# Start of a batched-experts kernel: x in three loads, and the identity and ScalarE's table load inside the Tile frame

## The chip, the cores and the metric

The kernel runs on one core of a Trainium2 chip. The metric is the device time of one execution in microseconds.

## The reference

Eight experts each have their own x (256 rows of 512), w1 (512 x 2048) and w2 (2048 x 512), all float32. Each expert is two matrix products with a relu between them:

```python
h = np.matmul(x, w1)        # x: (8, 256, 512), w1: (8, 512, 2048)
h = np.maximum(h, 0)
return np.matmul(h, w2).astype(np.float32)   # w2: (8, 2048, 512)
```

## The kernel before

The kernel is written by hand, engine by engine, with its own semaphores. Only its first instructions stand inside a Tile frame: a block that the Tile layer opens and that `tc.close()` ends (L97). At the end of the frame all five engines meet twice, and only then do they go on to the hand-written part. Inside the frame SP issues two loads of x, experts 0 and 1 (L92, first one) and experts 2 and 3 (second one), into `x_f` as float32. The name of each of these instructions is entered in `tc.no_tile_sem_insts`, so that the frame doesn't wait for them; they count up `s_x[0]` and `s_x[1]`.

After the frame:

- **GpSimd's queue (POOL)** issues everything that is cast on the way from float32 to bfloat16: first x of experts 4 to 7 into `x_c` (L139), then w1 of experts 0 and 1 (L129), then it makes the identity (memset L142, select L144, with the semaphore `s_id` between them and after them), then w2 of experts 0 and 1 (L134). w1 and w2 are double-buffered by expert; the later ones are issued when a half of the buffer is free (`s_first`, `s_act`). Last comes the store of experts 0 to 3 of the output (L163).
- **SP's queue**, after the x loads, waits for each weight to land and passes that on to TensorE as tokens (`t_w`, L113 to L121), and stores experts 4 to 6 (L123) and 7 (L125) of the output.
- **VectorE and ScalarE** first prepare x (`take_x`): in four rounds VectorE takes an even expert and ScalarE an odd one, copies it with its rows reordered into `x_b` as bfloat16 (`cast`, L174), waits for TensorE's transposes and copies these out of PSUM into `xe` (L190, and L193 for experts 4 to 7). ScalarE's first instruction here brings a load of its function table with it. Then both run `layers`: the relu out of PSUM into `ht` (L214, L216) and the copies of the output (L223).
- **TensorE** waits for the identity (`s_id`, L246), then makes four rounds of 16 transposes, each of which takes two tokens of `t_xb`, one from either cast. Then for each pair of experts it does the first products (L267) and the second ones (L287).

In `take_x` the wait for a load of x is by round:

```python
if r < G // 2:
    eng.wait_ge(s_x[r], 16)
```

Of the kernel before, what the change touches and what calls it, by code (L numbers as in the profile page):

```python
# [9 lines left out]
def kernel(  # L10
# [7 lines left out]
    nc = tc.nc  # L18
    P = 128
    bf = mybir.dt.bfloat16  # L20
    f32 = mybir.dt.float32
    relu = mybir.ActivationFunctionType.Relu
# [8 lines left out]
    G = E // 2  # L31
# [10 lines left out]
    x_r = x.rearrange("e (p m) k -> p e m k", m=MT)  # L42
# [3 lines left out]
    x_f = nc.alloc_sbuf_tensor("x_f", [P, G, MT, H], f32)  # L46
# [7 lines left out]
    w1_k = w1_sb[:, :2 * KT1 * F].rearrange("p (k n) -> p k n", n=F)  # L54
    w2_k = w2_sb[:].rearrange("p (k n) -> p k n", n=H)
    o_sb = nc.alloc_sbuf_tensor("out_sb", [P, E, MT, H], f32)
    identity = nc.alloc_sbuf_tensor("identity", [P, P], bf)
    ph = [nc.alloc_psum_tensor(f"pt_h{b}", [P, FB // 2, C], f32) for b in range(2)]
    po = nc.alloc_psum_tensor("pt_o", [P, MT, H], f32)
    pt = [nc.alloc_psum_tensor(f"pt_tr{b}", [P, KT1 * MT, P], bf) for b in range(2)]  # L60

    sem = nc.alloc_semaphore
    s_x = [sem(f"s_x{i}") for i in range(G // 2)]
    s_xc = sem("s_xc")
    s_out = [sem(f"s_out{i}") for i in range(3)]
    s_w1 = [sem(f"s_w1_{e}") for e in range(E)]
    s_w2 = [sem(f"s_w2_{e}") for e in range(E)]
    s_w2b = [sem(f"s_w2b_{e}") for e in range(E - 2, E)]
    s_id = sem("s_id")
    s_act = sem("s_act")  # L70
    s_dve = sem("s_dve")
    s_tr = sem("s_tr")
# [11 lines left out]
    sp, pool, act, dve, pe = nc.sync, nc.gpsimd, nc.scalar, nc.vector, nc.tensor  # L84
# [3 lines left out]

    def load_x(e, n, i):
        ins = sp.dma_start(x_f[:, e:e + n], x_r[:, e:e + n]).then_inc(s_x[i], 16)  # L92
        return ins.ins.name

    for r in range(G // 2):
        tc.no_tile_sem_insts.add(load_x(2 * r, 2, r))
    tc.close()  # L97
    tc.compile()  # L98

# [28 lines left out]
    def load_w1(e):  # L128
        pool.dma_start(w1_k[:, e % 2 * KT1:(e % 2 + 1) * KT1], w1_r[e]).then_inc(s_w1[e], 16)  # L129

    def load_w2(e):
        k = e % 2 * KT2
        if e < E - 2:
            pool.dma_start(w2_k[:, k:k + KT2], w2_r[e]).then_inc(s_w2[e], 16)  # L134
        else:
            pool.dma_start(w2_k[:, k:k + CUT], w2_r[e, :, :CUT]).then_inc(s_w2[e], 16)  # L136
            pool.dma_start(w2_k[:, k + CUT:k + KT2], w2_r[e, :, CUT:]).then_inc(s_w2b[e - E], 16)
# [1 line left out]
    pool.dma_start(x_c[:], x_rows).then_inc(s_xc, 16)  # L139
    load_w1(0)  # L140
    load_w1(1)
    pool.memset(identity[:], 0.0).then_inc(s_id, 1)  # L142
    pool.wait_ge(s_id, 1)
    pool.affine_select(  # L144
        out=identity[:],
        in_=identity[:],
        compare_op=mybir.AluOpType.not_equal,
        fill=1.0,
        base=0,
        pattern=[[-1, P]],  # L150
        channel_multiplier=1,
    ).then_inc(s_id, 1)
    load_w2(0)
    load_w2(1)
    for e in range(2, E, 2):
# [13 lines left out]
    def cast(eng, r, b):  # L169

        a = 2 * r + b
        src = x_f[:, a] if a < G else x_c[:, MT * (a - G):MT * (a - G + 1)]
        copy = act.copy if eng is act else dve.tensor_copy
        copy(  # L174
            x_b[:, b].rearrange("p (t m) q -> p t m q", m=MT),
            src.rearrange("p m (q t) -> p t m q", t=KT1),
        ).then_inc(t_xb, 1)

    def take_x(eng, b):
        copy = act.copy if eng is act else dve.tensor_copy  # L180
        for r in range(G):
            if r < G // 2:
                eng.wait_ge(s_x[r], 16)
            elif r == G // 2:
                eng.wait_ge(s_xc, 16)
            cast(eng, r, b)
            eng.wait_ge(s_tr, 2 * r + b + 1)
            a, n = 2 * r + b, KT1 * C
            if a < G:
                copy(xe[:, a * n:(a + 1) * n], pt[b][:].rearrange("p j q -> p (j q)")).then_inc(s_xe[b], 1)  # L190
            else:
                xl = xe[:, G * n:].rearrange("p (l j q f) -> p l j q f", l=G, j=KT1 * MT, f=G)
                copy(  # L193
                    xl[:, :, :, :, a - G].rearrange("p l j q -> p j l q"),
                    pt[b][:].rearrange("p j (l q) -> p j l q", l=G),
                ).then_inc(s_xe[b], 1)
# [28 lines left out]

    act.sem_inc(t_ha, 1)
    take_x(act, 1)
    layers(act, 1, s_ha, s_oa, t_ha, s_act)

    dve.sem_inc(t_hb, 1)  # L230
    take_x(dve, 0)
    layers(dve, 0, s_hb, s_ob, t_hb, s_dve)

# [9 lines left out]
            pe.lower_ap(aps[-1], for_matmul_weights=weights)  # L243
        return aps

    pe.wait_ge(s_id, 2)  # L246
    with pe.Fori(0, G) as _r:
        take(t_xb, 2)
        for b in range(2):
            for j in range(KT1 * MT):  # L250
                ins = pe.transpose(pt[b][:, j], x_b[:, b, j], identity[:])  # L251
            ins.then_inc(s_tr, 1)

    with pe.Fori(0, G) as g:
        with pe.Fori(0, 2) as b:
            xs = ahead(xe, False, g * (4 * KT1 * C) + b * (2 * KT1 * C), [kt * C for kt in range(KT1)], C)
            take(t_w)
            with pe.Fori(0, NQ) as q:
                for i in range(FB):
# [6 lines left out]
                    for kt in range(KT1):  # L266
                        ins = pe.matmul(  # L267
                            ph[i // 2][:, i % 2, :],
                            ws[i % 2 * KT1 + kt],
                            xs[kt],  # L270
                            start=(kt == 0),
                            stop=(kt == KT1 - 1),
                        )
                    if i % 2:
                        ins.then_inc((s_hb, s_ha)[i // 2], 1)
        with pe.Fori(0, 2) as b:
            for kt in range(KT2):
# [8 lines left out]
                for m in range(MT):  # L286
                    ins = pe.matmul(  # L287
                        po[:, m],
                        hs[(kt - k0) * MT + m],
                        ws[kt - k0],  # L290
                        start=(kt == 0),
                        stop=(kt == KT2 - 1),
                    )
# [35 lines left out]
```

## Time and profile before

| | before |
|---|---|
| median of 3 runs | 179.58 us (179.54 to 179.58) |
| profiled execution, its own time | 179.67 us |
| its span, first to last instruction | 178.4 us |
| mean granted TensorE clock | 0.963 of full |
| TensorE matmul busy | 131.5 us (74%) |
| VectorE, ScalarE, GpSimd busy | 37.3, 37.9, 12.4 us |
| read from and written to HBM | 71.30 MB and 4.19 MB, 423 GB/s over the span |
| share of the software DMA queue (GpSimd's) | 94.2% of the 16 DMA engines' span |

A row of the profile names an engine, a line of the kernel, an operation, and what it writes and reads (`x_f<-in_x_dram`); "PEq", "SPq" and the like are the sequencers of the engines. Times are microseconds from the first instruction. `w_sb` stands for both weight buffers, `pt_tr`, `pt_h` and `pt_o` for the PSUM tensors of the transposes, of the first and of the second products.

### The profile page before, as it was taken

Reading aid. Unit: us, or ns where it says so; the run is one execution under the profiler, and the core shown is the slowest. Engines: PE = TensorE matmul, PEld = TensorE weight load, DVE = VectorE, ACT = ScalarE, POOL = GpSimd, SP = SyncE. Lnnn points to the kernel's source line nnn. Section 1 sums busy time; section 2 is a strip of 40 time slices with the busy share of each in tenths; the row PEclk is TensorE's granted clock in tenths of the full one; section 3 lists DMA queues with packets and bytes.
Section 4 is the critical chain, followed back from the end, with each engine's and each line's share of the span. In section 5 each row is a group of like instructions: output and inputs, shape, how many; then the busy total and the mean of one; then the engine's idle time right before and its main releaser. Section 6 shows DMA issues by size and latency. Waiting matters only on the chain. (4 is left out here: it accounts for less than half of the span.)

```text
span 178.4 us, 2360 instructions
## 1 busy us (share of the span) xinstructions
PE 131.5 (74%) x832; PEld 89.3 (50%) x832; DVE 37.3 (21%) x48; ACT 37.9 (21%) x49; POOL 12.4 (7%) x26
## 2 busy tenths in 40 slices
PE   0214479899949696899769695979495695998950
PEld 0213368796413295794224485954142694953410
DVE  0232653332010133131100231320101141311010
ACT  2455554222010122121100132220101122311010
POOL 3500000101010101001000101010202100000000
PEclk9999999999987999699969999999999999999996
DMA  5999989989989989989999998998998999999998
GB/s 181 349 234 235 228 184 235 235 176 235 235 176 235 235 184 228 235 191 220 235 206 206 235 220 191 235 232 180 235 235 176 235 235 192 201 214 225 280 417 353
DMA packets 4352, 40.90 MB, mean 229 GB/s; under 512 B 384, under 2 KB 384, under 8 KB 2176
## 3 DMA queue, kind: packets, MB, share of 16 engines
q0 software_dynamic: 3264, 36.70, 94.2%
q1 hardware_dynamic: 1088, 4.19, 6.1%
HBM read 71.30 MB, written 4.19 MB: 423 GB/s over the span
## 5 line engine op out<-in xcount | busy, mean ns | idle before, releaser
L267 PE MATMUL pt_h<-xe,w_sb 128*128 x512 | 65.0, 284 | 12.9 <-PEq L87 12.9
L267 PEld LDWEIGHTS pt_h<-xe,w_sb 128*128 x512 | 57.5, 147 | 21.0 <-issue 19.2
L287 PE MATMUL pt_o<-w_sb,ht_sb 128*128 x256 | 59.7, 393 | 9.7 <-PEq L87 9.7
L287 PEld LDWEIGHTS pt_o<-w_sb,ht_sb 128*128 x256 | 25.3, 100 | 42.7 <-issue 16.2
L216 DVE TENSOR_SCALAR ht_sb<-pt_h 128x512 bf16<-128x512 f32 x32 | 22.1, 692 | 51.7 <-PE pt_h L267 51.6
L214 ACT ACTIVATE ht_sb<-pt_h 128x512 bf16<-128x512 f32 x32 | 19.1, 597 | 56.7 <-PE pt_h L267 56.7
L251 PE MATMUL pt_tr<-identity,x_b 128*128 128x128 bf16 x64 | 7.5, 309 | 17.7 <-PEq L87 17.7
L223 DVE COPY out_sb<-pt_o 128x512 f32 x8 | 5.5, 692 | 66.1 <-PE pt_o L287 66.1
L223 ACT COPY out_sb<-pt_o 128x512 f32 x8 | 4.7, 586 | 64.3 <-PE pt_o L287 64.3
L251 PEld LDWEIGHTS pt_tr<-identity,x_b 128*128 128x128 bf16 x64 | 6.5, 143 | 18.4 <-issue 18.4
L129 POOL DMA_DIRECT2D w_sb<-in_w_dram x8 | 4.3, 534 | 71.3 <-ACTq L218 71.3
L134 POOL DMA_DIRECT2D w_sb<-in_w_dram x6 | 3.9, 652 | 35.3 <-ACT out_sb L223 35.2
L193 DVE COPY xe<-pt_tr 128x1024 bf16<-128x1024 bf16 x2 | 4.9, 2466 | 5.2 <-PE pt_tr L251 5.2
L193 ACT COPY xe<-pt_tr 128x1024 bf16<-128x1024 bf16 x2 | 4.9, 2465 | 4.1 <-PE pt_tr L251 4.1
L174 ACT CAST x_b<-x_f 128x1024 bf16<-128x1024 f32 x2 | 4.0, 2000 | 2.9 <-DMA x_f<-in_x_dram 2.9
L174 DVE CAST x_b<-x_f 128x1024 bf16<-128x1024 f32 x2 | 2.2, 1076 | 7.9 <-DMA x_f<-in_x_dram 7.9
L190 ACT COPY xe<-pt_tr 128x1024 bf16<-128x1024 bf16 x2 | 2.0, 1012 | 4.1 <-PE pt_tr L251 4.1
L190 DVE COPY xe<-pt_tr 128x1024 bf16<-128x1024 bf16 x2 | 1.4, 692 | 4.2 <-PE pt_tr L251 4.2
L136 POOL DMA_DIRECT2D w_sb<-in_w_dram x2 | 1.1, 531 | 17.0 <-ACT out_sb L223 17.0
L174 ACT COPY x_b<-x_c 128x1024 bf16<-128x1024 bf16 x2 | 2.2, 1118 | 0.0
L174 ACT ACT_TABLE_LOAD x1 | 1.3, 1283 | 2.6 <-PEq L98 2.6
L174 DVE COPY x_b<-x_c 128x1024 bf16<-128x1024 bf16 x2 | 1.4, 700 | 0.0
(9 smaller groups left out, 3.4 us busy)
## 6 DMA issues: line engine op xcount, KB each, us to landing
w_sb<-in_w_dram POOLq DMA_DIRECT2D x14, 2048.0 KB, 29.5
w_sb<-in_w_dram POOLq DMA_DIRECT2D x2, 1152.0 KB, 26.7
x_f<-in_x_dram SPq DMA_DIRECT2D x2, 1024.0 KB, 7.7
out_dram<-out_sb POOLq DMA_DIRECT2D x1, 2048.0 KB, 36.0
w_sb<-in_w_dram POOLq DMA_DIRECT2D x2, 896.0 KB, 30.4
out_dram<-out_sb SPq DMA_DIRECT2D x1, 1536.0 KB, 8.6
x_c<-in_x_dram POOLq DMA_DIRECT2D x1, 1024.0 KB, 9.9
out_dram<-out_sb SPq DMA_DIRECT2D x1, 512.0 KB, 5.8
```

The source lines that it names most:

```text
L129: pool.dma_start(w1_k[:, e % 2 * KT1:(e % 2 + 1) * KT1], w1_r[e]).then_inc(s_w1[e], 16)
L134: pool.dma_start(w2_k[:, k:k + KT2], w2_r[e]).then_inc(s_w2[e], 16)
L136: pool.dma_start(w2_k[:, k:k + CUT], w2_r[e, :, :CUT]).then_inc(s_w2[e], 16)
L174: copy(x_b[:, b].rearrange("p (t m) q -> p t m q", m=MT), src.rearrange("p m (q t) -> p t m q", t=KT1),).then_inc(t_xb, 1)
L190: copy(xe[:, a * n:(a + 1) * n], pt[b][:].rearrange("p j q -> p (j q)")).then_inc(s_xe[b], 1)
L193: copy(xl[:, :, :, :, a - G].rearrange("p l j q -> p j l q"), pt[b][:].rearrange("p j (l q) -> p j l q", l=G),).then_inc(s_xe[b], 1)
L214: act.activation(dst, ph[half][:], relu).then_inc(t_h, 1)
L216: dve.tensor_relu(dst, ph[half][:]).then_inc(t_h, 1)
L223: copy(outs[b], po[:, half]).then_inc(s_copied, 1)
L251: ins = pe.transpose(pt[b][:, j], x_b[:, b, j], identity[:])
L267: ins = pe.matmul(ph[i // 2][:, i % 2, :], ws[i % 2 * KT1 + kt], xs[kt], start=(kt == 0), stop=(kt == KT1 - 1),)
L287: ins = pe.matmul(po[:, m], hs[(kt - k0) * MT + m], ws[kt - k0], start=(kt == 0), stop=(kt == KT2 - 1),)
```

## The change

SP issues three loads of x in the frame instead of two: expert 0 alone, expert 1 alone (128 rows of 4 KB each), and experts 2 and 3 together. In the first round VectorE waits for expert 0's load and ScalarE for expert 1's, in the second both wait for the third. In the frame ScalarE runs a relu on one column of a constant, `warm`, which brings the table load with it, and GpSimd makes the identity. The semaphore `s_id` and TensorE's wait for it are gone; the frame itself orders the select behind the memset, with a semaphore that Tile allocates. In the built program that semaphore is cleared by GpSimd between the two meetings at the frame's end, and SP waits for it there.

```diff
+    warm = nc.alloc_sbuf_tensor("warm", [P, 1], f32)
...
-    s_x = [sem(f"s_x{i}") for i in range(G // 2)]
+    s_x = [sem(f"s_x{i}") for i in range(3)]
...
-    s_id = sem("s_id")
...
+    def own(ins):
+        tc.no_tile_sem_insts.add(ins.ins.name)
+
     def load_x(e, n, i):
-        ins = sp.dma_start(x_f[:, e:e + n], x_r[:, e:e + n]).then_inc(s_x[i], 16)
-        return ins.ins.name
-
-    for r in range(G // 2):
-        tc.no_tile_sem_insts.add(load_x(2 * r, 2, r))
+        own(sp.dma_start(x_f[:, e:e + n], x_r[:, e:e + n]).then_inc(s_x[i], 16))
+
+    for i, (e, n) in enumerate(((0, 1), (1, 1), (2, 2))):
+        load_x(e, n, i)
+    act.activation(warm[:], nc.const_aps.tensor(1.0, [P, 1], f32), relu)
+    pool.memset(identity[:], 0.0)
+    pool.affine_select(
+        out=identity[:],
+        in_=identity[:],
+        compare_op=mybir.AluOpType.not_equal,
+        fill=1.0,
+        base=0,
+        pattern=[[-1, P]],
+        channel_multiplier=1,
+    )
     tc.close()
     tc.compile()
...
     load_w1(0)
     load_w1(1)
-    pool.memset(identity[:], 0.0).then_inc(s_id, 1)
-    pool.wait_ge(s_id, 1)
-    pool.affine_select(
-        ...
-    ).then_inc(s_id, 1)
     load_w2(0)
     load_w2(1)
...
             if r < G // 2:
-                eng.wait_ge(s_x[r], 16)
+                eng.wait_ge(s_x[b if r == 0 else 2], 16)
...
-    pe.wait_ge(s_id, 2)
     with pe.Fori(0, G) as _r:
```

More of the change, by code (lines that the diff above doesn't have):

```diff
@@ L141 @@
     load_w1(1)
-    pool.memset(identity[:], 0.0).then_inc(s_id, 1)
-    pool.wait_ge(s_id, 1)
[L144 to L151, printed above, removed]
-    ).then_inc(s_id, 1)
     load_w2(0)
```

## The prediction

> **What bounds the kernel now.** The page comes first: how busy each engine is, how busy the DMA engines are, and what the queues carried.
>
> ```profile
> span 178.4 us, 2360 instructions
> PE 131.5 (74%) x832; PEld 89.3 (50%) x832; DVE 37.3 (21%) x48; ACT 37.9 (21%) x49; POOL 12.4 (7%) x26
> DMA  5999989989989989989999998998998999999998
> q0 software_dynamic: 3264, 36.70, 94.2%
> HBM read 71.30 MB, written 4.19 MB: 423 GB/s over the span
> w_sb<-in_w_dram POOLq DMA_DIRECT2D x14, 2048.0 KB, 29.5
> ```
>
> TensorE is busy for three quarters of the span, the DMA engines for nearly all of it. To see whether they ever stand still, I cut the span where the traffic changes (the columns after the stretch are its length, the five engines, the granted clock, the DMA share and GB/s written at the destination; a weight is read as float32 and written as bfloat16, so its GB/s count half of what is read).
>
> ```profile
> 0.00:1.70 1.70, 0.00 (x0) 0.00 (x0) 0.00 (x0) 0.00 (x0) 0.20 (x4) 1.00 0.00 0
> 1.70:2.70 1.00, 0.00 (x0) 0.00 (x0) 0.00 (x0) 0.15 (x1) 0.00 (x0) 1.00 0.84 70
> 2.70:6.80 4.10, 0.00 (x0) 0.00 (x0) 1.09 (x1) 2.31 (x2) 3.44 (x6) 1.00 1.02 421
> 6.80:7.60 0.80, 0.00 (x0) 0.00 (x0) 0.00 (x0) 0.80 (x1) 0.57 (x2) 1.00 1.14 307
> 7.60:12.40 4.80, 1.86 (x16) 1.63 (x16) 1.31 (x2) 1.67 (x3) 0.00 (x0) 1.00 1.03 234
> 12.40:168.30 155.90, 126.13 (x801) 86.26 (x802) 34.17 (x45) 32.40 (x45) 8.18 (x15) 0.97 1.02 217
> 168.30:177.60 9.30, 3.54 (x17) 1.40 (x15) 0.69 (x1) 0.59 (x1) 0.00 (x0) 0.88 1.02 420
> 177.60:178.40 0.80, 0.00 (x0) 0.00 (x0) 0.00 (x0) 0.00 (x0) 0.00 (x0) 0.50 0.09 36
> ```
>
> From 2.7 to 177.6 us the share is 1.02 or more in every stretch: there is no hole. The 155.9 us in the middle are the 16 weight matrices, so one takes 9.74 us; the page's 29.5 us from issue to landing are three of those, that is, each matrix is queued about 20 us before its turn. Nothing that TensorE, VectorE or ScalarE does by a microsecond or two earlier or later reaches the weight stream. At the end the writes of the output run at 420 GB/s to 0.8 us before the end of the span. So the time is: when the DMA engines start, plus any hole in their work, plus a fixed amount of bytes. A step of the change counts only if it moves the start (1.8 us) or opens a hole.
>
> **The change part by part.** All of it lies in the first eight microseconds. This is the timeline there (start, duration, engine, line, operation), and the issue durations of the x loads and of the two output stores that SP issues:
>
> ```profile
> 0.74 0.95 SPq L92 DMA_DIRECT2D x_f<-in_x_dram  x2
> 2.55 1.28 ACT L174 ACT_TABLE_LOAD   x1 [2.55 <-PEq L98]
> 2.99 0.68 POOL L139 DMA_DIRECT2D x_c<-in_x_dram  x1 [2.54 <-POOLq L98]
> 3.66 1.07 POOL L129 DMA_DIRECT2D w_sb<-in_w_dram  x2
> 4.70 0.24 POOL L142 MEMSET identity<- 128x128 bf16 x1
> 5.18 0.28 POOL L144 TENSOR_SCALAR_AFFINE_SELECT identity<-identity 128x128 bf16<-128x128 bf16 x1 [0.24 <-POOL identity L142]
> 5.63 2.01 ACT L174 CAST x_b<-x_f 128x1024 bf16<-128x1024 f32 x1 [1.79 <-DMA x_f<-in_x_dram]
> 5.63 1.09 DVE L174 CAST x_b<-x_f 128x1024 bf16<-128x1024 f32 x1 [5.63 <-DMA x_f<-in_x_dram]
> L92 SPq DMA_DIRECT2D x_f<-in_x_dram x2: 433/446/459, 0.7 to 1.2; - x2
> 168.48 0.39 SPq L123 DMA_DIRECT2D out_dram<-out_sb  x1
> 172.49 0.36 SPq L125 DMA_DIRECT2D out_dram<-out_sb  x1
> ```
>
> *Three x loads for two.* The bytes are the same. Expert 0 arrives alone after 0.52 MB instead of with expert 1 after 1.05 MB, at 421 GB/s some 1.25 us sooner, so VectorE's cast starts near 4.4 instead of 5.63. That gains nothing by itself: TensorE's first transposes take two casts, and ScalarE's, on expert 1, still starts when expert 1 has landed, near 5.6, and takes 2.01 us. The start of traffic stays: the first issue still begins at 0.74. Its duration could shrink from 433 ns to the 0.36 us of L125, which has 128 rows, so data could come 0.07 us sooner; but L123 with 384 rows takes 0.39, less than the 256-row loads, so the row count isn't what sets it. I take 0, bounds -0.07 and +0.05 (the end marks of one more transfer).
>
> *The frame's end moves.* SP issues three loads before it reaches the end of the Tile frame, at which all engines meet. Now it is through at 0.74 + 0.95 = 1.69, and GpSimd's x_c load is issued at 2.99, 1.30 us behind it. A third issue costs 0.36 (L125) to 0.48 us (half of 0.95): SP is through at 2.05 to 2.17.
>
> *The table load in the frame.* ScalarE now loads after the frame (2.55 to 3.83), and then idles 1.79 us for x_f, so nothing is won by moving it. In the frame it begins with SP's first issue, near 0.74, takes 1.28, and the one-column activation follows. The nearest rows for that:
>
> ```profile
> L190 ACT COPY xe<-pt_tr 128x1024 bf16<-128x1024 bf16 x2 | 2.0, 1012 | 4.1 <-PE pt_tr L251 4.1
> L223 ACT COPY out_sb<-pt_o 128x512 f32 x8 | 4.7, 586 | 64.3 <-PE pt_o L287 64.3
> L214 ACT ACTIVATE ht_sb<-pt_h 128x512 bf16<-128x512 f32 x32 | 19.1, 597 | 56.7 <-PE pt_h L267 56.7
> ```
>
> 512 columns more cost 426 ns, so one column costs about 586 - 426 = 160 ns; at most it is the 597 of a whole ACTIVATE. ScalarE reaches the frame's end at 0.74 + 1.28 + 0.16 = 2.18 (at most 2.62): level with SP.
>
> *The identity in the frame.* GpSimd's memset to the end of the select takes 4.70 to 5.46, 0.76 us; in the frame it ends near 1.5, well before SP. Behind the frame 0.9 us of GpSimd's time between the w1 and w2 issues goes away. The w2 load that is then issued sooner has its turn behind x_c and two w1, after 12.4 + 2 x 9.74 = 31.9 us: worth nothing. TensorE loses its wait for the identity, which had passed long before the casts ended (7.64). In the built program the identity makes the frame use a semaphore of its own, and GpSimd clears that between the two meetings at the frame's end while the others arrive there; I take 0 for it, bounds 0 and 0.1 (one of its const memsets takes 0.1).
>
> *Sum for GpSimd's queue.* The x_c load is issued 0.36 to 0.58 us later; I take 0.5, at 3.49. With ScalarE at its bound it would be 0.93 + 0.1. What hides this is the x traffic of SP's queue. Packets and MB by queue, first up to 6.8 us (no packet of the software queue is in that answer), then from 6.8 to 7.2, then up to 13:
>
> ```profile
> q1 hardware_dynamic: 454, 1.79, 74.1%
> ...
> q0 software_dynamic: 12, 0.10, 117.0%
> ...
> q1 hardware_dynamic: 544, 2.10, 44.9%
> ```
>
> At 6.8 us SP's loads have 2.10 - 1.79 = 0.31 MB to go, which at 421 GB/s last 0.74 us, to 7.54. In the profile shown x_c's first packets start at 6.8, 3.81 us behind their issue. If that lag stays, they start at 7.30 now (7.16 to 7.38; at the far bound 7.83). 7.30 is before 7.54: the DMA engines work through, with x_f first and x_c after it instead of mixed. **Hole: 0** (far bound 7.83 - 7.54 = 0.29). If the cover were gone, the whole 0.5 us would show in the time.
>
> The sum against the profiled execution: its own time is 179.67 us, span 178.4 and 1.27 around it; plus 0 for the start, 0 for the hole, and 0 for all that hangs behind the weights. That execution stands 0.09 above the median of the runs shown, 179.58, so I give 179.6. The likeliest case alone spans 179.5 to 179.9 (-0.07 for the start; +0.29 for the hole).
>
> **A rule that speaks against the change.** VectorE's cast now begins at 4.4, when GpSimd is just done with x_c's descriptors (3.49 + 0.68 = 4.17) and at work on w1's. That this matters is seen in one row, the w2 issues, whose first, at 5.59, lies beside the cast of 5.63 to 6.72:
>
> ```profile
> 5.59 1.78 POOL L134 DMA_DIRECT2D w_sb<-in_w_dram  x2
> L134 POOL DMA_DIRECT2D w_sb<-in_w_dram x6: 531/531/1248, 5.6 to 100.0; - x6
> ```
>
> One of six took 1248 ns instead of 531, and 5.59 + 1.25 = 6.84, 0.12 us behind the end of the cast: the issue stood still while VectorE cast. Here w1 is what stands still, to about 4.4 + 1.09 + 0.12 = 5.6, and its turn is at 12.4, so I cost it at nothing. The Trainium skill ("SBUF — State Buffer", section "SBUF: two separate sides") states that GpSimd can't write descriptors while VectorE holds their shared port in a 2-port mode, and that a float32 tensor_copy within SBUF triggers it; by that rule, and on the times above, the sum stays as it is, as long as x_c's descriptors are written first. The trace's 1248 ns agree with it.
>
> **The rivals.** *Slower: the cast catches x_c's descriptors.* If x_c's issue slips 0.9 us rather than 0.5 (ScalarE at its bound of 0.93 does it), it is still being written when the cast starts at 4.4; the point of decision is a slip of 0.7 (2.99 + 0.68 + 0.7 = 4.4). Then it ends at 5.6 instead of 3.67, the first packets come at 5.6 + (6.8 - 3.67) = 8.7, and the hole is 8.7 - 7.54 = 1.2 us: 180.8 us. For it: the 1248 ns and the small margin, 0.2 us by my sum. Against it: x_c's first packets at 6.8 stand so close to the end of the cast, 6.72, that the lag of 3.8 us may itself be partly this wait, in which case an earlier cast releases x_c earlier.
>
> *Slower: ScalarE holds the frame's end.* If the frame's end has to wait after a table load as long again as the load itself, ScalarE arrives at 0.74 + 2 x 1.28 + 0.16 = 3.46, 1.77 later than SP does now; x_c's packets start at 6.8 + 1.77 = 8.57, the hole is 1.0: 180.6 us. The trace can't tell: after its load ScalarE idles 1.79 us for x_f anyway. The Trainium skill ("ScalarE: Activation LUTs", section "What ACT_TABLE_LOAD costs") gives 1283 ns for the load, as the trace has it, and a drain of about 1380 ns behind it, which no row here shows; if that drain were additional, an estimate from its figures is a hole of 1.1 us.
>
> *Faster: the first data come sooner.* From the first issue to data are 1.8 - 0.74 = 1.06 us. If that were proportional to the rows of the transfer, 128 instead of 256 would save 0.5 us, and every byte behind would come as much sooner: 179.1. Against it, 384 rows are issued in 0.39 and 128 in 0.36.
>
> *The change does nothing at all:* the frame's end might not move, if SP's issues overlap with it. That is 179.6 too.
>
> **How the numbers follow.** 0.2% is 0.36 us, about what a measurement of this kernel can tell from no change. The forecast and the case that nothing moves, both inside it: 0.62. The cast catching x_c: 0.16. ScalarE at the frame's end: 0.06. A lag or slip beyond my bounds without either of these, hole 0.4 to 0.9: 0.07. First data sooner: 0.09. So faster 0.09, same 0.62, slower 0.16 + 0.06 + 0.07 = 0.29. The range runs from 179.2, leaving out most of the faster case, to 180.8, which holds the two slower rivals; it is wide because one cause of 0.2 us can turn a hidden slip into a hole of a microsecond.
>
> **What would show it.** Right: SP's three issues end near 2.1; the table load starts near 0.74; x_c is issued near 3.5; the expert 0 cast starts near 4.4 and ScalarE's near 5.6; no stretch from 2.7 us to the last 0.8 us has a DMA share clearly under 1; the last ACT copy of the tail (now 171.88) stays within 0.3 us. Wrong: x_c's issue lasting clearly over 0.68 us, or x_c's first packets later than 7.6 with a low DMA share before them, and the first weight matmul of each later expert late by the same amount; or x_f data before 1.5 us.

## The result, and the profile after

| | before | changed |
|---|---|---|
| median of 12 runs | 179.6 us (179.45 to 179.96) | 180.23 us (179.53 to 181.22) |
| ratio, 95% interval | | 1.0037 (1.0021 to 1.0053) |
| profiled execution: time, span | 179.67, 178.4 us | 181.06, 179.7 us |

The changed kernel is 0.37% slower (0.2 to 0.5), 0.63 us by the medians; the forecast was 179.6, no change. The median hides what happens: six of the twelve runs lie between 179.53 and 179.86 like the kernel before, the other six between 180.59 and 181.22. The profiled execution is one of the slower six.

The page of the changed kernel, in the lines that answer to those of before:

```profile
span 179.7 us, 2356 instructions
DMA  5999999999999999999999999999999999999996
q0 software_dynamic: 3264, 36.70, 93.5%
HBM read 71.30 MB, written 4.19 MB: 420 GB/s over the span
x_f<-in_x_dram SPq DMA_DIRECT2D x1, 1024.0 KB, 8.1
x_c<-in_x_dram POOLq DMA_DIRECT2D x1, 1024.0 KB, 11.1
```

The bytes are the same, and at this grain the DMA row shows nothing. Its start, in the timeline:

```profile
0.74 0.20 POOL L100 MEMSET identity<- 128x128 bf16 x1 [0.29 <-POOLq L314]
0.74 1.28 ACT L99 ACT_TABLE_LOAD   x1 [0.74 <-PEq L314]
0.74 1.34 SPq L95 DMA_DIRECT2D x_f<-in_x_dram  x3
1.02 0.29 POOL L101 TENSOR_SCALAR_AFFINE_SELECT identity<-identity 128x128 bf16<-128x128 bf16 x1
2.04 0.20 ACT L99 ACTIVATE warm<-const-float32-1.0 128x1 f32<-128x1 f32 x1
3.48 0.67 POOL L152 DMA_DIRECT2D x_c<-in_x_dram  x1 [2.18 <-POOLq L111]
4.12 1.07 DVE L176 CAST x_b<-x_f 128x1024 bf16<-128x1024 f32 x1 [4.12 <-DMA x_f<-in_x_dram]
4.15 1.69 POOL L142 DMA_DIRECT2D w_sb<-in_w_dram  x2
5.33 1.99 ACT L176 CAST x_b<-x_f 128x1024 bf16<-128x1024 f32 x1 [3.09 <-DMA x_f<-in_x_dram]
```

Each of these times is where the prediction put it, within 0.3 us. What it missed is in the windows (stretch, length, five engines, granted clock, DMA share, GB/s):

```profile
2.30:3.40 1.10, 0.00 (x0) 0.00 (x0) 0.00 (x0) 0.00 (x0) 0.00 (x0) 1.00 1.01 402
3.40:4.60 1.20, 0.00 (x0) 0.00 (x0) 0.48 (x1) 0.00 (x0) 1.12 (x2) 1.00 1.04 427
4.60:5.40 0.80, 0.00 (x0) 0.00 (x0) 0.59 (x1) 0.07 (x1) 0.80 (x2) 1.00 0.57 205
5.40:6.60 1.20, 0.00 (x0) 0.00 (x0) 0.00 (x0) 1.20 (x1) 1.20 (x3) 1.00 0.79 304
6.60:7.40 0.80, 0.00 (x0) 0.00 (x0) 0.00 (x0) 0.72 (x1) 0.29 (x1) 1.00 1.02 328
```

Three of the same cuts of the kernel before:

```profile
2.30:3.40 1.10, 0.00 (x0) 0.00 (x0) 0.00 (x0) 0.85 (x1) 0.41 (x1) 1.00 0.68 276
4.60:5.40 0.80, 0.00 (x0) 0.00 (x0) 0.00 (x0) 0.00 (x0) 0.56 (x3) 1.00 1.05 430
5.40:6.60 1.20, 0.00 (x0) 0.00 (x0) 0.97 (x1) 0.97 (x1) 1.07 (x2) 1.00 1.02 420
```

There is a hole from 4.6 to 6.6 us: share 0.57 and then 0.79, 205 and 304 GB/s instead of 430 and 420. At 4.6 us the first two x loads have used up their bytes, and the third isn't there yet on many of the DMA engines: by the packets in the trace, about half of the 16 are moving a row at 5.0 us, where in the kernel before all are. Lost are 0.8 x 225 + 1.2 x 116 = 319 KB, 0.76 us at 420 GB/s; a sooner start gave back 1.1 x 126 = 139 KB. The mean loss is smaller than the time, because every transfer is complete only when the slowest DMA engine has done its part, and the holes are not shared evenly: x_c lands at 3.48 + 11.1 = 14.6 us instead of 2.99 + 9.9 = 12.9, 1.7 us later. The 9.9 is in the page of the kernel before:

```profile
x_c<-in_x_dram POOLq DMA_DIRECT2D x1, 1024.0 KB, 9.9
```

Thirteen of the 16 parts of x_c land by 13.6 us, the other three at 14.4 to 14.6; in the kernel before all sixteen land at 12.7 to 12.9. The delay of the latest three goes on nearly unchanged through all weights to the last copies of the output, first in the changed kernel, then in the kernel before:

```profile
166.40 7.07 PE L288 MATMUL pt_o<-w_sb,ht_sb 128*128 x31 [0.79 <-PEq L87]
173.50 0.58 ACT L225 COPY out_sb<-pt_o 128x512 f32 x1 [7.27 <-PE pt_o L288]
```

```profile
171.88 0.59 ACT L223 COPY out_sb<-pt_o 128x512 f32 x1 [7.27 <-PE pt_o L287]
```

173.50 against 171.88 is 1.62 us; the span is 1.3 longer.

### The profile page after: what moved, and what is told of

Read it like the earlier page. It is cut to its first block, busy times and chain, and to the rows that moved or that the text cites. A ratio compares the mean times of both kernels' runs of the same rounds, so it can differ in the third digit from the quotient of the medians.

```text
span 179.7 us, 2356 instructions
## 1 busy us (share of the span) xinstructions
PE 134.7 (75%) x824; PEld 91.2 (51%) x832; DVE 37.3 (21%) x48; ACT 37.9 (21%) x50; POOL 12.3 (7%) x26
## 5 line engine op out<-in xcount | busy, mean ns | idle before, releaser
L268 PE MATMUL pt_h<-xe,w_sb 128*128 x512 | 68.1, 293 | 12.6 <-PEq L87 12.5
L268 PEld LDWEIGHTS pt_h<-xe,w_sb 128*128 x512 | 59.4, 148 | 22.1 <-issue 18.9
## 6 DMA issues: line engine op xcount, KB each, us to landing
x_c<-in_x_dram POOLq DMA_DIRECT2D x1, 1024.0 KB, 11.1
```

The source lines that it names most:

```text
L268: ins = pe.matmul(ph[i // 2][:, i % 2, :], ws[i % 2 * KT1 + kt], xs[kt], start=(kt == 0), stop=(kt == KT1 - 1),)
```

## The experiments

Each is an edit of the changed kernel unless it says otherwise. The ratios are to the kernel before, timed beside them.

**VectorE's cast late.** Is it the third load, VectorE's early cast, or the later frame end?

```diff
-                eng.wait_ge(s_x[b if r == 0 else 2], 16)
+                if r == 0:
+                    eng.wait_ge(s_x[0], 16)
+                eng.wait_ge(s_x[1 if r == 0 else 2], 16)
```

> The changed kernel, but VectorE waits for experts 0 and 1 both before its first cast, so that the cast starts near 5.3 us instead of 4.1; the three x loads and the frame stay. Theory A (the third x load reaches some DMA engines late because it is the third one outstanding in SP's queue): the hole in the DMA work at 4.6 to 6.6 us stays, runs scatter from 179.5 to 181.2, median near 180.2. Theory B (VectorE's early cast, beside GpSimd's descriptor writing, makes the hole): no hole, share 1.0 from 2.3 us on, times 179.2 to 179.6 with little scatter. Theory C (the later frame end and x_c issue make it): as in A.

Median 180.53 us (179.72 to 181.14, six of eight runs over 180), ratio 1.0041 (1.0021 to 1.0061). The cast starts at 5.43 and the hole stays; these are windows of this kernel:

```profile
4.60:5.00 0.40, 0.00 (x0) 0.00 (x0) 0.00 (x0) 0.00 (x0) 0.40 (x2) 1.00 0.60 195
5.00:5.40 0.40, 0.00 (x0) 0.00 (x0) 0.00 (x0) 0.00 (x0) 0.40 (x2) 1.00 1.01 225
```

That is 195 and 225 GB/s where the kernel before has 430. The share of 1.01 beside 225 GB/s isn't full work: by the packets in the trace, nine rows that begin between 5.0 and 5.6 us take 0.42 to 1.11 us each, where most take 0.16. So the early cast is not the cause.

**One and three experts.**

```diff
-    for i, (e, n) in enumerate(((0, 1), (1, 1), (2, 2))):
+    for i, (e, n) in enumerate(((0, 1), (1, 3))):
...
-                eng.wait_ge(s_x[b if r == 0 else 2], 16)
+                eng.wait_ge(s_x[b if r == 0 else 1], 16)
```

> The changed kernel with two x loads instead of three: expert 0 alone, experts 1 to 3 together. VectorE's first cast stays early (near 4.1 us), ScalarE's first cast moves to near 7.8. Theory A: only two loads, no hole, 179.2 to 179.6. Theory B: the early cast still lies beside GpSimd's descriptor writing, hole near 4.6 to 6.6 us, scatter up to 181. Theory C: x_c's issue goes back to near 3.0 us, no hole.

179.6 us (179.49 to 179.87), ratio 0.9997 (0.9989 to 1.0006). The early cast (4.14) and the table load in the frame stay; with two loads there is no slow half. My line on x_c's issue was wrong: it is at 3.43, not 3.0, though SP is through at 1.61, 0.47 us sooner than with three loads.

**Two loads as before, the rest in the frame.**

```diff
-    for i, (e, n) in enumerate(((0, 1), (1, 1), (2, 2))):
+    for i, (e, n) in enumerate(((0, 2), (2, 2))):
...
-                eng.wait_ge(s_x[b if r == 0 else 2], 16)
+                eng.wait_ge(s_x[r], 16)
```

> The changed kernel with the two x loads of the kernel before (experts 0 and 1, experts 2 and 3); identity and table load stay in the frame. Theories A and B: no hole, 179.6 like the kernel before, since the first full DMA rate is back at 2.7 us and the cast back at 5.6. Theory C: the frame's part alone shows, if ScalarE or the semaphore clear hold the frame's end: x_c issued at 3.2 or later, and a slower median by 0.1 to 0.6.

179.71 us (179.51 to 179.95), ratio 1.0003 (0.9994 to 1.0012): the frame's part costs nothing that shows. But it does move the frame's end:

```profile
0.74 1.28 ACT L99 ACT_TABLE_LOAD   x1 [0.74 <-PEq L314]
0.74 0.95 SPq L95 DMA_DIRECT2D x_f<-in_x_dram  x2
2.04 0.20 ACT L99 ACTIVATE warm<-const-float32-1.0 128x1 f32<-128x1 f32 x1
3.42 0.67 POOL L152 DMA_DIRECT2D x_c<-in_x_dram  x1 [2.12 <-POOLq L111]
```

SP is through at 1.69, as before; ScalarE ends at 2.24, and x_c is issued 1.18 us behind that, at 3.42 instead of 2.99. The frame's part alone moves x_c's issue by 0.43 us, and x_f's traffic hides it, as the prediction's sum had it.

**Three loads alone**, the other half of the change put on the kernel before:

```diff
-    for r in range(G // 2):
-        tc.no_tile_sem_insts.add(load_x(2 * r, 2, r))
+    for i, (e, n) in enumerate(((0, 1), (1, 1), (2, 2))):
+        tc.no_tile_sem_insts.add(load_x(e, n, i))
...
-                eng.wait_ge(s_x[r], 16)
+                eng.wait_ge(s_x[b if r == 0 else 2], 16)
```

> The kernel before with only the x loads changed to three (expert 0, expert 1, experts 2 and 3); identity and table load stay behind the frame. Theories A and B: the hole at 4.6 to 6.6 us and the scatter up to 181.2, median near 180.2, as in the changed kernel. Theory C: no hole, 179.2 to 179.6.

180.66 us (179.69 to 181.03, eight of twelve over 180), ratio 1.0038 (1.0022 to 1.0055): the whole of the change's loss. A window shows the same hole:

```profile
4.60:5.00 0.40, 0.00 (x0) 0.00 (x0) 0.40 (x1) 0.00 (x0) 0.40 (x1) 1.00 0.42 154
```

**The third load from ScalarE's queue.**

```diff
-    for i, (e, n) in enumerate(((0, 1), (1, 1), (2, 2))):
+    for i, (e, n) in enumerate(((0, 1), (1, 1))):
...
     act.activation(warm[:], nc.const_aps.tensor(1.0, [P, 1], f32), relu)
+    own(act.dma_start(x_f[:, 2:4], x_r[:, 2:4]).then_inc(s_x[2], 16))
```

> The changed kernel, but the third x load (experts 2 and 3) is issued by ScalarE's queue, in the frame behind the table load (near 2.3 us), instead of SP's. Theory L (a queue keeps two loads going, the third starts about a microsecond or more after the first has landed): no queue has more than two, so no hole at 4.6 to 6.6 us, times 179.4 to 179.8. Theory S (a load needs 2.6 to 4.5 us from its issue to its data under traffic, and the two short loads before it cover only to 4.7): issued 0.6 us later than by SP, the hole stays or grows, median 180.2 or more.

179.53 us (179.46 to 179.69), ratio 0.9991 (0.9982 to 1.0): no hole. But the load wasn't issued behind the table load, as I had expected:

```profile
0.81 0.44 ACTq L100 DMA_DIRECT2D x_f<-in_x_dram  x1
```

ScalarE's sequencer issued it at 0.81 while the table was being loaded. So it was there early, and this run says that a second queue cures the hole, not whether the cure is the queue or the earlier issue. Its trace shows something more: from 4.2 to 5.1 us every packet is of ScalarE's load, 0.35 MB, and none of SP's second load, whose issue was over at 1.60 and whose forerunner had landed by 4.45. So here even the second load comes a while behind its turn; whether it was late or had to wait for the other queue, the trace doesn't tell, but the other queue's traffic fills the time.

**Four loads of one expert.**

```diff
-    for i, (e, n) in enumerate(((0, 1), (1, 1), (2, 2))):
+    for i, (e, n) in enumerate(((0, 1), (1, 1), (2, 1), (3, 1))):
...
-                eng.wait_ge(s_x[b if r == 0 else 2], 16)
+                eng.wait_ge(s_x[2 * r + b], 16)
```

> The changed kernel with four x loads of one expert each. Theory L: the third starts late as before (hole from 4.6 us) and the fourth again waits for the second, so the hole is as large or larger, median 180.2 to 181. Theory S: the fourth is issued near 2.1 us and has arrived by 6.6, so one hole as in the changed kernel, median near 180.2 to 180.5. If neither, no hole: 179.6. The frame's end also moves by 0.45 us, x_c issued near 3.9.

180.82 us (180.34 to 180.93, all five runs slow), ratio 1.0056 (1.0042 to 1.0069), but by another cause than either theory's. From its timeline and its windows:

```profile
3.94 1.54 POOL L152 DMA_DIRECT2D x_c<-in_x_dram  x1 [2.64 <-POOLq L111]
4.30 1.06 DVE L176 CAST x_b<-x_f 128x1024 bf16<-128x1024 f32 x1 [4.30 <-DMA x_f<-in_x_dram]
```

```profile
7.40:12.40 5.00, 1.86 (x16) 1.62 (x16) 1.67 (x2) 2.96 (x3) 0.20 (x1) 1.00 0.89 184
```

At 4.6 us nothing like the hole of the changed kernel is seen (369 GB/s from 4.6 to 5.4). The fourth issue moves x_c's to 3.94, VectorE's cast starts at 4.30 while its descriptors are written, the issue lasts 1.54 us instead of 0.67, and the hole comes where x_f ends. This is the prediction's slower rival, which the change as made just misses (x_c's issue is over at 4.15, the cast starts at 4.12, and it lasted 0.67).

**Four loads, cast late.** To see whether that is it, the cast was made to wait for expert 1 as well:

```diff
-                eng.wait_ge(s_x[2 * r + b], 16)
+                if r == 0:
+                    eng.wait_ge(s_x[0], 16)
+                eng.wait_ge(s_x[1 if r == 0 else 2 + b], 16)
```

> Four x loads of one expert each as in the run before it, but VectorE's first cast waits for expert 1 too and so starts near 5.4 us, behind x_c's descriptors (issue near 3.9 to 4.6). If the cast that caught x_c's descriptors was what made that run slow (its x_c issue lasted 1.54 us instead of 0.67): x_c's issue takes 0.67 again, x_c lands near 13 on all DMA engines, 179.5 to 179.8. If four loads are slow by themselves: 180.3 to 180.9 again.

179.66 us (179.51 to 180.76), ratio 1.0011 (0.9998 to 1.0024).

```profile
3.94 0.68 POOL L152 DMA_DIRECT2D x_c<-in_x_dram  x1 [2.64 <-POOLq L111]
5.45 1.07 DVE L176 CAST x_b<-x_f 128x1024 bf16<-128x1024 f32 x1 [5.45 <-DMA x_f<-in_x_dram]
```

```profile
7.40:12.40 5.00, 1.87 (x16) 1.63 (x16) 1.67 (x2) 2.93 (x3) 0.00 (x0) 1.00 1.13 238
```

Its timeline and window show that the issue is at 3.94 as before, takes 0.68 again, and the hole behind it is gone: by the medians the collision is worth 180.82 - 179.66 = 1.16 us (the kernel before had a median of 179.70 beside both). But four of the twelve runs lie at 180.01 to 180.76: third and fourth loads of 128 rows may still be late at times. None of these four was profiled, so that isn't shown.

**Two, one and one expert; one, two and one.** Three loads, with the long one first or in the middle (waits to match):

```diff
-    for i, (e, n) in enumerate(((0, 1), (1, 1), (2, 2))):
+    for i, (e, n) in enumerate(((0, 2), (2, 1), (3, 1))):
```

> The changed kernel with three x loads in another order of size: experts 0 and 1 together, then expert 2, then expert 3. The third is issued at 1.7 us as in the changed kernel and needed near 6.4. Theory L: the first lands near 5.6, so the third starts at 6.3 to 8: a hole from 6.4, partly filled by x_c's packets from 7.3 on; median 179.8 to 180.5. Theory S: 2.6 to 4.5 us from its issue it is there (4.3 to 6.2), so no hole, 179.6.

179.72 us (179.57 to 180.22), ratio 1.0005 (0.9996 to 1.0014); ten of eleven runs show no loss, and the eleventh wasn't profiled. The hole that theory L as I had put it (third load at 6.3 to 8 us) called for is not there.

```diff
-    for i, (e, n) in enumerate(((0, 1), (1, 1), (2, 2))):
+    for i, (e, n) in enumerate(((0, 1), (1, 2), (3, 1))):
```

> The changed kernel with three x loads: expert 0, then experts 1 and 2 together, then expert 3. The second lasts until about 6.0 us. Theory L: the first lands near 4.1, the third starts from 4.7 to 6.6: covered by the second but for the latest DMA engines, median 179.6 to 179.9. Theory S: the same. If any third load costs a fixed hole: 180.2 or more.

179.55 us (179.37 to 179.84), ratio 0.9993 (0.9984 to 1.0002). Three loads as such cost nothing. With the second load lasting until about 6, the third is in time in every run, and the sooner start is kept: the interval just reaches 1, so a gain isn't shown.

**Halves.** Meant to tell theory L from a limit on the rows in the queue:

```diff
-    for i, (e, n) in enumerate(((0, 1), (1, 1), (2, 2))):
-        load_x(e, n, i)
+    for i in range(2):
+        h = slice(64 * i, 64 * i + 64)
+        own(sp.dma_start(x_f[h, 0:1], x_r[h, 0:1]).then_inc(s_x[i], 16))
+    load_x(1, 1, 2)
+    load_x(2, 2, 3)
```

> The changed kernel with the first load in two halves of 64 rows (expert 0), then expert 1, then experts 2 and 3; VectorE's first cast waits for the first three. Theory L (two loads of a queue at a time): the third waits for the first half, hole from 3.5 us, and again from 4.7; DMA share clearly under 1 at 3.5 to 4.0. Theory K (a queue holds a limited number of rows, 34 marks per DMA engine and not 35, so that the last load of 256 rows waits for room): nothing at 3.5, the last load waits only for the first half, which is over near 2.9, so a small hole or none at 4.7; time 179.5 to 180.0.

181.07 us (180.54 to 181.85), ratio 1.0073 (1.0047 to 1.0099), and inconclusive, since with the halves the traffic behind the first 0.5 us is slow by itself:

```profile
2.30:3.40 1.10, 0.00 (x0) 0.00 (x0) 0.00 (x0) 0.00 (x0) 0.00 (x0) 1.00 0.77 231
3.40:4.60 1.20, 0.00 (x0) 0.00 (x0) 0.00 (x0) 0.00 (x0) 0.18 (x1) 1.00 1.00 222
```

A share of 1.00 at 222 GB/s is no hole, but DMA engines that are busy and move half as much: a row that begins between 3.4 and 4.6 us takes some 0.25 to 0.32 us instead of 0.16. The 231 GB/s of the first window, at a share of 0.77, are the start-up: from 2.7 to 3.2 us the first half itself runs at 369.

**The changed kernel twice more**, for its profile:

> The changed kernel again, for a second profile. If the hole at 4.6 to 6.6 us is what makes the scatter: a time near 181 with the hole, or a time of 179.5 to 179.9 without it.

> The changed kernel once more, for a third profile; the same expectation as the run before.

One came out slow, 181.12 us, one quick, 179.58. First the slow one, by windows and by the issues of its page (the last column is the time from issue to landing):

```profile
4.60:5.40 0.80, 0.00 (x0) 0.00 (x0) 0.53 (x1) 0.11 (x1) 0.80 (x2) 1.00 1.00 312
5.40:6.60 1.20, 0.00 (x0) 0.00 (x0) 0.00 (x0) 1.20 (x1) 1.20 (x3) 1.00 0.94 369
```

```profile
x_f<-in_x_dram SPq DMA_DIRECT2D x1, 1024.0 KB, 13.8
x_c<-in_x_dram POOLq DMA_DIRECT2D x1, 1024.0 KB, 11.2
```

The quick one, by the same two views:

```profile
4.60:5.40 0.80, 0.00 (x0) 0.00 (x0) 0.69 (x1) 0.00 (x0) 0.80 (x2) 1.00 1.05 420
5.40:6.60 1.20, 0.00 (x0) 0.00 (x0) 0.00 (x0) 1.14 (x1) 1.20 (x4) 1.00 1.01 416
```

```profile
x_f<-in_x_dram SPq DMA_DIRECT2D x1, 1024.0 KB, 6.6
x_c<-in_x_dram POOLq DMA_DIRECT2D x1, 1024.0 KB, 9.5
```

The quick one has no hole at all; its third x load is complete 6.6 us after the issue, and x_c 9.5. In the slow one they take 13.8 and 11.2. The hole is smaller on average here than in the first profile (312 and 369 GB/s against 205 and 304), yet the time is the same: it falls on fewer DMA engines (12 or 13 of the 16 are moving a row at 5.0 us, against about half), and the latest one counts.

The landing that counts is that of x_c. In all fourteen profiles the time of the execution goes with it: x_c lands (issue plus time to landing) at 12.7 to 13.1 us in the eight that took 179.56 to 179.69, at 14.0 in the one of 180.46, at 14.4 to 14.7 in the four of 180.93 to 181.12, and at 15.0 in the one of 181.45. The landing of x_f isn't such a sign: in the kernel before its last part lands at 11.78, in the changed kernel's first profile at 9.76.

## Why the prediction was right or wrong

The range, 179.2 to 180.8, holds the median of 180.23, but by luck: its upper part was there for two rivals that did not come about, and the likeliest case, no change, had no term for what did.

**What bounds it** was right. The time followed the DMA engines in every profile, and VectorE's cast 1.5 us sooner (4.12 for 5.63) or the first transposes (7.46 for 7.78) brought nothing.

**The frame's end** was right in its size: x_c's issue at 3.48 (forecast 3.49), SP through at 2.08 (2.05 to 2.17), ScalarE at 2.24 (2.18), the identity at 1.31 (1.5). The frame's part by itself moves x_c's issue by as much (3.42 with two loads) as the third issue does (3.40 with three loads alone); they cover each other. I took the frame's semaphore at 0 with a bound of 0.1. Where SP is the last to arrive, x_c's issue follows it by 1.39 us with the identity in the frame (four loads, 2.55 to 3.94) and by 1.30 and 1.32 without, which would be 0.07 to 0.09 for it. Moved into the frame, neither the table load nor the identity shows in the time (1.0003).

**"Hole: 0" was wrong, and the step that failed is "Three x loads for two".** I counted the bytes and the issue times, and took it that SP's queue would flow on from the second load to the third as it does from the first to the second. The only row for such a passage was that one. With three loads the second passage comes at 4.6 us, and there the queue ran dry in half of the runs: in the mean of the DMA engines 0.76 us of work, on the slowest enough to delay x_c by 1.7 us. I priced one more transfer at +0.05 at most; it costs up to 1.6 us, 0.63 in the medians. I looked for the hole only where x_f ends, at 7.54, and there it isn't: in the quick profile x_c's first packets come at 7.23, forecast 7.30. That the lag behind the issue would stay was right there by luck, for it isn't fixed: it is 3.75 us in that profile, 3.28 in the late-cast kernel with four loads, and 4.03 in the changed kernel's first profile.

**The start** was mis-sized in bytes: I took 0 with a bound of -0.07. A first load of 128 rows reaches 402 GB/s between 2.3 and 3.4 us where one of 256 rows has 276, worth 139 KB or 0.33 us. First data come at nearly the same time; they get up to rate sooner. Over the profiles it is 343 to 410 GB/s with 128 rows and 257 to 294 with 256. But no run shows this in the time: the quick profile took 179.58 us, and its x_c landed at 13.0, no sooner than in the kernel before (12.9). The faster rival's reason was half right, and its 0.5 us did not come.

**The slower rivals.** VectorE's cast catching x_c's descriptors is real, and its price is near the one that I had worked out (1.16 us measured, 1.2 forecast), but it was not the cause here: x_c's issue kept its 0.67 us. The price is partly luck: with four loads x_c's first packets come at 7.20, not at 8.7, but the first dozen of them then take 0.9 to 2.1 us each where 0.62 is usual. I put the point of decision at a slip of 0.7 us. A slip of 0.5 escapes and 0.95 (four loads) is caught, but the cast started at 4.12 and not at 4.4, which moves the point to 4.12 - 3.67 = 0.45: the change stood on it, with no margin. The collision showed itself where it costs nothing, in w1's issue (4.15, two in 1.69 us instead of 1.07), as forecast. The Trainium skill ("SBUF — State Buffer", section "A bandwidth-pool intuition that's wrong (but worth ruling out)") has GpSimd blocked until VectorE's end and about 115 ns more; with four loads x_c's issue ends at 3.94 + 1.54 = 5.48, 0.12 behind the end of the cast at 5.36, in agreement.

ScalarE holding the frame's end beyond its load is refuted: the activation starts at 2.04, 0.02 behind the load's end. The drain of about 1380 ns that the Trainium skill ("ScalarE: Activation LUTs", section "What ACT_TABLE_LOAD costs") puts behind a load is not an addition here: x_c's issue follows ScalarE's end by 1.18 us in the two-load run, no more than it follows SP's (1.30) in the kernel before. The drain that the program holds there runs from 0.81 to 2.26 in that trace, beside the load.

**What stays open** is why the third load is late. Shown: the loss comes with a third load in SP's queue behind two of 128 rows, and not from the cast, the frame, or three loads as such. How often a run is slow goes with how much traffic the second load gives between the end of the first and the third's turn: with 0.52 MB, some 1.25 us, the third load is late in 6 of 12, 6 of 8 and 8 of 12 runs when it has 256 rows, in 4 of 12 and 1 of 11 when it has 128; with 1.05 MB it was in time in 11 of 11. (Runs over 180 us are counted as late; of those with a third load of 128 rows none was profiled.) Where SP's queue was alone, a second load never cost time, though its turn comes sooner behind its issue (issued near 1.2 us, its turn near 3.5 where 0.52 MB go ahead of it) than that of the third (1.7 and 4.6). A race fits another sign: VectorE's and ScalarE's first casts, which wait for the two short loads, start at 4.22 and 5.46 in the quick profile, and at 4.12 and 5.33, 4.07 and 5.29, and 4.01 and 5.22 (three loads alone) in slow ones; the slower the short loads, the less hole. Most of this would fit a queue that gets the third load going only when the first has ended, and then needs about the 1.06 us that the first load takes from issue to data: with 1.25 us of cover it is a race. That the long load first and then two short ones, with the same cover, was slow in only 1 of 11 runs speaks against so simple a rule. And no run separates it from a limit on the rows in the queue, or from a lag that merely varies.

## What to carry to other kernels

When the DMA engines set the time, every passage from one transfer to the next is a place where they can run dry, and a split that leaves bytes and issue times alone can still open a hole: give the transfers in the middle enough bytes to cover the start of the next, or have another queue's traffic there to cover it. Look at the share in stretches of a microsecond with the GB/s beside it, since rows that stand still count as busy, and at when the transfer that leads the rest of the stream lands, because the slowest DMA engine, not the mean, delays all that follows. When the times of a kernel fall into two groups, take profiles until each group has one.

## What the runs showed of the hardware

- With a third load of 256 rows behind two of 128 rows in one DMA queue, 20 of 32 runs took over 180 us. In the profiled ones of these the third load came late with its issue long done (SP through at 2.08 us, the hole from 4.6), and x_c behind it landed up to 1.8 us later than in the kernel before.
- With two loads of 64 rows into 64 partitions each, the DMA engines moved 222 GB/s from 3.4 to 4.6 us at a share of 1.00, with loads of 128 rows 427. The Trainium skill ("SBUF — State Buffer", section "Door 1: The DMA port swizzle (why `[64,N]` ≈ `[32,N]`)") states that 64 partitions in a row reach half of the ports. The 222 GB/s fit that; the 369 GB/s of the first half between 2.7 and 3.2 us do not, so the run shows the loss but not its cause.
- ScalarE's queue issued a load at 0.81 us while its table was being loaded (0.74 to 2.02).
